# Small work handed out between the blocks of a dense product, and indexer scores on whole 128-row tiles, in a kernel of two small transformers

## The chip, the core and the metric

The kernel runs on one core of a Trainium2 chip, as one program. The metric is the device time of one execution in microseconds. Times of the kernel before and of the changed kernel are medians of several runs. The engines are named as in the profile: PE (TensorE matmul), PEld (its weight loads), DVE (VectorE), ACT (ScalarE), POOL (GpSimd), SP (SyncE, which issues the weight loads from memory).

## The reference

512 tokens of width 1024 in float32 go through two small models, one after the other. The first has two layers: a mixer of convolution and causal attention, a gated linear recurrence, and after each a squared-ReLU MLP of width 4096. The second puts 16 learned meta tokens ahead (528 tokens) and has two layers, each with a hybrid mixer and a gated MLP of width 2816. Only the hybrid mixer is touched in its own code:

```python
def hybrid_mixer(n, w_in, ...):
    proj = n @ w_in          # 528 x 3408 columns
    aq, ak, av, az, aa, ab, bq, bk, bv, iq, ik, iw = jnp.split(proj, SPLIT_POINTS, axis=-1)
    o_a = gated_deltanet(aq, ak, av, az, aa, ab, ...)        # 4 heads of 128, a chunked recurrence
    o_b = dsa_attention(bq, bk, bv, iq, ik, iw, ...)
    gates = sigmoid(n @ w_gate + b_gate)
    return (gates_a * (o_a @ w_branch_a) + gates_b * (o_b @ w_branch_b)) @ w_out

# in dsa_attention: the indexer's scores pick 128 of the real keys for each query
    logit_i = jnp.einsum('bqhd,bsd->bhqs', iqb, ik_r)         # 8 heads of 64
    score = jnp.einsum('bhqs,bqh->bqs', relu(logit_i), iwb)
    _, sel = lax.top_k(score, topk)                           # topk = 128
    p = softmax(concat([s_meta, s_sel]))                      # the 16 meta keys are always seen
    o = p[..., :N_META] @ v_m + p[..., N_META:] @ v_sel
```

## The kernel before

Activations stand with the 128 rows of a block of features on the partitions and the tokens along the free axis. Every dense product is cut into blocks of 128 output columns. Each weight block of 1024 x 128 is loaded by SP's queue into `wraw`, rounded to a short form `whi` by a cast on ACT (L99), and the rest is kept as `wlo` by a subtract on DVE (L100); `whi` and `wlo` have two buffers each. One block of a product over 1024 rows is then 8 steps of 128 rows (the loop over `k` in `products`, L145), each with three matmuls: `whi` by the high part of the activations, `whi` by their low part, `wlo` by the high part. With 528 tokens each matmul is done in two halves, so a block has 48 matmul instructions. Two PSUM tiles `mm` hold running blocks. The evacuation of a block (`evac`) frees its tile.

Around the dense blocks stands small work. Three lists hold it: `fill` (pairs of a cost and a step), `soon`, and `pending`. `product_done` is called once at the end of each block: it runs steps of `fill` until the block's `budget` is spent, then `soon` and one of `pending`, then the evacuation. `issue_after` ties the PE instructions of a step behind a given matmul; instructions of other engines are not tied. The order written here is a rank, not the queue: a planner builds each engine's queue from the ranks with its own modelled times, taking the first in rank that is ready, and the engines then run their queues strictly in order.

The hybrid mixer (`mixer_2`, run twice, called the late mixers here) goes through these stretches:

1. Four blocks of indexer queries (`ev_iq`: an ACT copy, a rotation on DVE L708 to L710, a split into `iq`), then the block of 80 small columns (L814), whose evacuation feeds the indexer's keys. In the first late mixer the normalisation of the stage before ends here too: `sums` (L260), `bc` and `bc1` are one `pending` step each, with a long chain of small DVE instructions and a spread by PE from `diag` (L284).
2. The block of k (`ev_qk`), four of q and one of v. The indexer's keys are turned and split (`keys`, L859, into `ikT[0]` and the low part `ikT[1]`), and `scores` (L880 to L887) come as `fill`: for each of three tiles of queries and each of 8 heads one matmul over 128 rows (L880) and one over the 64 rows that hold the low part (L881), a ReLU on ACT, a multiply-add on DVE.
3. Twelve blocks of the recurrence's q, k and v (`ev_a`: 5 DVE instructions of 528 columns), while `select` (17 steps for each of three tiles; L999 finds the eight largest, L1001 strikes them out, a chain on DVE) and the attention (`attend`) come as `fill` with a budget of 2 a block. What is left is run by `flush`.
4. Four blocks of z and sixteen of gates with the recurrence's preparation (`dn_keys`, `dn_prep`, `dn_solve`, `pair1` to `pair4`), one entry of `steps` a block.
5. The recurrence itself, the two branches, and the output product.

In the attention's `att_values` the 16 meta keys are one matmul of 16 rows (L1067) ahead of the real keys' matmuls of 128 rows (L1070). `squares` sums a block's columns by ten matmuls with one column each (L769).

## Time and profile before

| | |
|---|---|
| three runs, median | 2953.84 us |
| lowest and highest of them | 2943.05 and 2955.46 us |
| the profiled execution, its own time | 2948.39 us |
| its span in the profile | 2946.5 us |
| mean granted TensorE clock | 0.978 |

The profiled execution is one more run. The span is what the trace covers, from the first instruction to the last; 1.9 us of the execution's time lie around it. A granted clock of 1 is TensorE's upper level of 2.4 GHz, 0.5 its lower level of 1.2 GHz, and a number between is a mix of the two over the stretch. The busy time of PE is modelled and holds matmuls that overlap or run slowly, so the distance from start to start says more than the length of one.

### The profile page before, as it was taken

What the parts mean: (1) busy time and instruction counts of PE and PEld (TensorE: products, weight loads), DVE (VectorE), ACT (ScalarE), POOL (GpSimd) and SP (SyncE); (2) the same over time, 40 slices, a digit from 0 to 9 for tenths busy, and PEclk for the clock granted to TensorE, in tenths of its full rate; (3) what the DMA queues carried; (4) which work ended last, traced back from release to release, by engine and by line L of the source; (5) the groups of instructions that cost most, each with busy time, mean ns of one, the idle gap of its engine ahead of it and who ended that gap; (6) DMA issues with size and microseconds to landing.
All of it is one profiled execution on the core that took longest, in us unless ns stands there. A gap on an engine that the chain in (4) does not pass through costs nothing.

```text
span 2946.5 us, 44576 instructions
## 1 busy us (share of the span) xinstructions
PE 2849.4 (97%) x18009; PEld 2505.8 (85%) x18009; DVE 1856.0 (63%) x3462; ACT 1044.0 (35%) x1939; POOL 14.1 (0%) x117
## 2 busy tenths in 40 slices
PE   7999999999999998998999999999999999999999
PEld 5767888877888887888998999999788998988897
DVE  7986535468653557699747564555788757565563
ACT  3444222345321233353633322223444633332222
POOL 0000000000000000000000000000000000000000
PEclk9999999999999999799999999999998999999999
DMA  4214333332333334121354232324221253432333
GB/s 123 65 33 121 93 100 94 100 93 72 99 94 96 98 97 116 45 68 51 109 132 148 86 93 80 101 85 123 58 58 51 82 146 111 116 92 85 104 89 91
DMA packets 509860, 272.23 MB, mean 92 GB/s; under 512 B 40112, under 2 KB 494918, under 8 KB 509398
## 3 DMA queue, kind: packets, MB, share of 16 engines
q1 hardware_dynamic: 493520, 245.24, 29.5%
q10 hardware_dynamic: 16134, 24.14, 2.5%
q8 instruction: 142, 2.33, 0.3%
q14 instruction: 64, 0.52, 0.1%
HBM read 249.11 MB, written 20.23 MB: 91 GB/s over the span
## 4 chain that ended last, share of the span: by engine, by line
PE 87%; DVE 8%; DMA 2%; ACT 1%; issue 1%; SPq 0%; ACTq 0%; DVEq 0%
PE mm L145 74%; PE mm L1449 2%; DVE wlo L100 1%; PE b L1070 1%; PE b L769 1%; PE a L398 1%; PE a L881 1%; DMA qkv<-xz 1%; DVE ac L708 1%; DMA ax<-gd 1%; PE c L423 1%; DVE m L999 1%; DVE ac L971 1%; PE b L1067 1%; PE a L1027 1%
## 5 line engine op out<-in xcount | busy, mean ns | idle before, releaser
L145 PE MATMUL mm<-xparts,whi 128*128 128x256 f32 (+1 forms) x6752 | 1428.5, 320 | 16.8 <-ACT whi L99 7.8
L145 PEld LDWEIGHTS mm<-xparts,whi 128*128 128x128 f32 x6752 | 1045.6, 191 | 115.6 <-issue 9.5
L99 ACT CAST whi<-wraw 128x1024 fp32r<-128x1024 f32 (+1 forms) x472 | 457.8, 970 | 1405.9 <-PE mm L145 1167.8
L145 PE MATMUL mm<-xparts,wlo 128*128 128x256 f32 (+3 forms) x3376 | 888.2, 320 | 11.6 <-DVE wlo L100 11.6
L100 DVE TENSOR_TENSOR wlo<-wraw,whi 128x1024 fp32r<-128x1024 f32 (+1 forms) x472 | 529.3, 1121 | 411.3 <-ACT whi L99 404.9
L145 PEld LDWEIGHTS mm<-xparts,wlo 128*128 128x128 f32 x3376 | 565.4, 191 | 61.8 <-DVE wlo L100 16.7
L145 PE MATMUL mm<-hh,whi 128*128 128x512 f32 (+2 forms) x1040 | 340.1, 354 | 0.0
L145 PE MATMUL mm<-hh,wlo 128*128 128x512 f32 (+2 forms) x1040 | 339.9, 354 | 0.0
L145 PE MATMUL mm<-hl,whi 128*128 128x512 f32 (+2 forms) x1040 | 339.1, 353 | 0.0
L145 PEld LDWEIGHTS mm<-hl,whi 128*128 128x128 f32 x1040 | 184.3, 188 | 27.5
L145 PEld LDWEIGHTS mm<-hh,wlo 128*128 128x128 f32 x1040 | 183.8, 188 | 27.9
L145 PEld LDWEIGHTS mm<-hh,whi 128*128 128x128 f32 x1040 | 184.0, 188 | 26.4
L1449 PE MATMUL mm<-xparts,whi 128*128 128x256 f32 (+2 forms) x512 | 87.6, 289 | 9.2 <-DVE ax L1463 5.0
L507 DVE TENSOR_TENSOR down<-mm,r 128x512 f32<-128x512 f32 x32 | 22.1, 692 | 106.8 <-PE mm L145 106.8
L366 DVE SCALAR_TENSOR_TENSOR val<-z,cw,val 128x512 f32<-128x512 f32 x120 | 84.8, 746 | 0.5
L1449 PEld LDWEIGHTS mm<-xparts,whi 128*128 128x128 f32 x512 | 71.9, 190 | 11.5 <-issue 5.7
L1501 DVE TENSOR_TENSOR fx<-mm,rbc 128x528 f32<-128x528 f32 (+1 forms) x44 | 30.7, 702 | 76.4 <-PE mm L145 76.4
L1514 DVE TENSOR_TENSOR fc<-fc,mm 128x528 f32<-128x528 f32 (+1 forms) x44 | 30.6, 696 | 73.4 <-PE mm L145 73.4
L1102 DVE TENSOR_TENSOR ac<-mm,rbc 128x528 f32<-128x528 f32 (+1 forms) x32 | 22.4, 699 | 77.7 <-PE mm L145 77.7
L145 PE MATMUL mm<-qkv,whi 128*128 128x256 f32 (+2 forms) x384 | 67.6, 284 | 0.0
L1506 DVE SCALAR_TENSOR_TENSOR fc<-fx,vcols,fc 128x528 f32<-128x528 f32 (+1 forms) x88 | 66.1, 757 | 1.4
L1508 ACT ACTIVATE fx<-fc 128x528 f32<-128x528 f32 (+1 forms) x44 | 28.1, 639 | 88.9 <-DVE fc L1506 88.8
(532 smaller groups left out, 3144.0 us busy)
## 6 DMA issues: line engine op xcount, KB each, us to landing
wraw<-in_w_up SPq DMA_DIRECT2D x152, 512.0 KB, 4.0
wraw<-in_w_down SPq DMA_DIRECT2D x96, 512.0 KB, 4.3
wraw<-in_w_in SPq DMA_DIRECT2D x52, 512.0 KB, 3.8
wraw<-in_w_gate SPq DMA_DIRECT2D x32, 512.0 KB, 4.2
wraw<-in_ab_w_in SPq DMA_DIRECT2D x20, 512.0 KB, 3.8
wraw<-in_c_w_in SPq DMA_DIRECT2D x16, 512.0 KB, 3.9
wraw<-in_w_out SPq DMA_DIRECT2D x16, 512.0 KB, 4.8
wraw<-in_w_down SPq DMA_DIRECT2D x32, 192.0 KB, 2.6
```

The costliest lines, as they stand in the source:

```text
L99: self.S.copy(hi[:, :n], raw[:, :n])
L100: self.V.tensor_tensor(lo[:, :n], raw[:, :n], hi[:, :n].bitcast(F32), op=ALU.subtract)
L145: ins = self.PE.matmul(o, lhsT=wt[:, k % chunk, :], rhs=xt[:, t0:t1], start=n == 0, stop=n == 3 * kb - 1)
L366: V.scalar_tensor_tensor(cacc[b], z[b][:, j:j + S], w, cacc[b], op0=ALU.mult, op1=ALU.add)
L398: PE.matmul(ps[:, :W], lhsT=qk[p][r0:r0 + 64, P * i:P * i + P], rhs=qk[4 + p][r0:r0 + 64, :W], start=True, stop=True)
L423: PE.matmul(po[:, 64 * j:64 * j + 64], lhsT=pts[:, P * c:P * c + P], rhs=vt[c][:, h:h + 64], start=c == 0, stop=c == i)
L708: self.V.tensor_tensor(t[o], raw[i], tab[1][i], op=ALU.mult)
L769: PE.matmul(p5[:n, i:i + 1], lhsT=q[:, t0:t0 + n], rhs=self.ones[:, 0:1], start=True, stop=True)
L1449: PE.matmul(o, lhsT=wt[:, k, :], rhs=xt[:, m0 + t0:m0 + t1], start=k == 0 and j == 0, stop=k == 3 and j == 2)
L1501: V.tensor_tensor(x[:, 2:2 + TG], ps, self.rbc, op=ALU.mult)
L1506: V.scalar_tensor_tensor(c, x[:, d + j:TG + j], w(j), c, op0=ALU.mult, op1=ALU.add)
L1514: V.tensor_tensor(c, c, ps, op=ALU.mult)
```

## The change

- `products` now calls `run_fill` after each of the 8 steps of 128 rows instead of once a block, with an eighth of the block's budget. What a step costs beyond its share is carried over as a debt (`credit`), and no more than one share is saved up. Before, each block began anew and the last step could overshoot freely.
- The budgets are set anew: 4.8 a block in the stretch of k, q and v, in which a score costs 1; 4 instead of 2 in the stretch with the selections. An entry of the preparation is cut into its parts, and `dn_prep` into four.
- The cast and the subtract of a weight block get a rank 150 instructions earlier (`high_priority`).
- The low part of the indexer's keys stands in two tiles of 128 rows of which one half is zero (`ikT[1]`, `ikT[2]`), so that L881 takes 128 rows. The meta keys' transposes and matmuls take 128 rows, with zeros in `vt` (tiles of real queries alone). Column sums and transposes of the 16 meta tokens take 128 columns, which saves some small copies.
- The four indexer blocks become two, the block of 80 columns, and two. The block of k comes after them and now has a budget. `bc1` comes one block later, by an empty entry in `pending`.

The core of the diff:

```diff
+AHEAD = 150
@@ weight
-        self.S.copy(hi[:, :n], raw[:, :n])
-        self.V.tensor_tensor(lo[:, :n], raw[:, :n], hi[:, :n].bitcast(F32), op=ALU.subtract)
+        with self.tc.high_priority(AHEAD):
+            self.S.copy(hi[:, :n], raw[:, :n])
+            self.V.tensor_tensor(lo[:, :n], raw[:, :n], hi[:, :n].bitcast(F32), op=ALU.subtract)
@@ products, at the end of each step k
+                self.run_fill(ins, budget / kb)
@@ product_done
         with self.tc.issue_after(ins.ins):
-            self.run_fill(budget)
             for f in soon:
                 f()
@@
-    def run_fill(self, budget):
-        while self.fill and budget > 0:
+    def run_fill(self, ins, budget):
+        self.credit = min(self.credit + budget, budget)
+        while self.fill and self.credit > 0:
             cost, step = self.fill.pop(0)
-            budget -= cost
-            step()
+            self.credit -= cost
+            with self.tc.issue_after(ins.ins):
+                step()
@@ turn_end
-        self.pending = [sums, bc, bc1] + [lambda k=k: final(k) for k in range(0, KB, 2)]
+        self.pending = [sums, bc, lambda: None, bc1] + [lambda k=k: final(k) for k in range(0, KB, 2)]
@@ mixer_2
-                    V.tensor_copy(out[:, :4], p5[:, :4])
-                    V.tensor_copy(out[:META, 4:5], p5[:META, 4:5])
+                    V.tensor_copy(out, p5[:, :5])
...
-            self.dense(w_in[:, 2824:3336], self.xparts, T2, ev_iq, early=True, lag=4)
+            self.dense(w_in[:, 2824:3080], self.xparts, T2, ev_iq, early=True, lag=4)
...
-            self.dense(w_in[:, 2568:2696], self.xparts, T2, ev_qk("k_norm", 4, [kT]))
+            self.dense(w_in[:, 3080:3336], self.xparts, T2, ev_iq, first=2, early=True)
...
-                self.split(ps, *ikT)
-            self.fill.append((99, lambda: None))
-            self.fill.append((0.5, keys))
+                S_.copy(ikT[0], ps)
+                for i in range(2):
+                    o = slice(64 * i, 64 * i + 64)
+                    V.tensor_tensor(ikT[1 + i][o], ps[o], ikT[0][o].bitcast(F32), op=ALU.subtract)
+            BS_ = 4.8
+            self.fill.append((BS_, lambda: None))
+            self.fill.append((1, keys))
+            self.fill.append((2, lambda: None))
...
-                PE.matmul(ps[:, :W], lhsT=q[r0:r0 + 64], rhs=ikT[1][r0:r0 + 64, :W], start=False, stop=True)
+                PE.matmul(ps[:, :W], lhsT=q, rhs=ikT[1 + h % 2][:, :W], start=False, stop=True)
...
-                    self.fill.append((0.25 + 0.14 * i, lambda i=i, h=h: scores(i, h)))
-            self.dense(w_in[:, 2056:2568], self.xparts, T2, ev_qk("q_norm", 0, qT), budget=4.5)
-            self.dense(w_in[:, 2696:2824], self.xparts, T2, ev_v, budget=4.5)
+                    self.fill.append((1, lambda i=i, h=h: scores(i, h)))
+            self.dense(w_in[:, 2568:2696], self.xparts, T2, ev_qk("k_norm", 4, [kT]), budget=BS_)
+            self.dense(w_in[:, 2056:2568], self.xparts, T2, ev_qk("q_norm", 0, qT), budget=BS_)
+            self.dense(w_in[:, 2696:2824], self.xparts, T2, ev_v, budget=BS_)
...
-                    PE.matmul(po[:, j, :], lhsT=vt[:META, 4, :], rhs=tm[:, :n], start=True, stop=W == META)
+                    PE.matmul(po[:, j, :], lhsT=vt[:META if W == META else P, 4, :], rhs=tm[:, :n], start=True, stop=W == META)
...
-                self.dense(col(w_in, b), self.xparts, T2, ev_a, first=b, budget=2)
+                self.dense(col(w_in, b), self.xparts, T2, ev_a, first=b, budget=4)
...
-            steps += [[lambda t=t: dn_prep(*t)] for t in tiles[1:]]
-            steps.append([lambda: dn_prep(*tiles[0]), dn_solve])
+            gens = [dn_prep(*t) for t in tiles]
+            part = lambda i: lambda: next(gens[i], None)
+            steps += [[part(i)] * 4 for i in range(1, 5)]
+            steps.append([part(0)] * 4 + [dn_solve])
...
-                    self.fill.append((1, lambda k=k: [f() for f in steps[k]]))
+                    self.fill.extend((1 / len(steps[k]), f) for f in steps[k])
```

## Rows read from the trace of the kernel before

**Rows 1.** The page, part 1: each engine's busy time over the whole span.

```profile
PE 2849.4 (97%) x18009; PEld 2505.8 (85%) x18009; DVE 1856.0 (63%) x3462; ACT 1044.0 (35%) x1939; POOL 14.1 (0%) x117
```

**Rows 2.** Windows: stretch, length, busy time per engine (instructions), granted clock, DMA share, GB/s.

```profile
1128.60:1179.70 51.10, 44.35 (x317) 40.87 (x318) 41.00 (x82) 16.25 (x27) 0.98 (x5) 0.87 0.43 126
1179.70:1254.20 74.50, 73.65 (x400) 59.79 (x398) 47.57 (x124) 27.42 (x52) 0.79 (x5) 0.79 0.16 43
1254.20:1343.00 88.80, 83.86 (x643) 77.87 (x641) 82.88 (x199) 45.91 (x103) 1.00 (x10) 1.00 0.22 60
1343.00:1400.00 57.00, 50.92 (x353) 46.76 (x353) 51.36 (x106) 18.88 (x41) 0.00 (x0) 0.91 0.20 56
1750.00:1800.00 50.00, 50.00 (x415) 50.00 (x414) 27.84 (x38) 13.56 (x16) 0.40 (x4) 1.00 0.25 74
2047.20:2090.10 42.90, 38.94 (x309) 37.00 (x308) 34.07 (x60) 15.85 (x25) 0.46 (x7) 1.00 0.34 89
2090.10:2159.50 69.40, 68.97 (x399) 55.79 (x397) 47.50 (x124) 27.23 (x52) 0.86 (x5) 0.85 0.17 46
```

**Rows 3.** Timeline of PE, first products of the first late mixer: start, length.

```profile
1155.49 2.04 PE L284 MATMUL a<-diag,ones 128*128 128x512 f32 x2 [1.02 <-DVE diag L271]
1160.83 0.81 PE L145 MATMUL mm<-xparts,wlo 128*128 128x256 f32 x2 [3.30 <-DVE wlo L100]
```

**Rows 4.** Timeline of PE, the indexer's scores of the first late mixer.

```profile
1200.12 0.28 PE L880 MATMUL a<-ikT,iq 128*128 128x256 f32 x1
1200.34 0.38 PE L881 MATMUL a<-ikT,iq 64*128 64x256 f32 x1
1200.65 0.39 PE L145 MATMUL mm<-xparts,whi 128*128 128x256 f32 x1
1233.05 0.39 PE L880 MATMUL a<-ikT,iq 128*128 128x512 f32 x1
1233.37 0.61 PE L881 MATMUL a<-ikT,iq 64*128 64x512 f32 x1
```

**Rows 5.** Windows of three stalls and their ends, columns as in rows 2.

```profile
1148.70:1160.80 12.10, 5.43 (x11) 2.07 (x10) 11.67 (x24) 3.32 (x7) 0.21 (x2) 0.62 0.00 0
1349.00:1356.40 7.40, 7.40 (x31) 6.54 (x32) 6.61 (x16) 1.16 (x4) 0.00 (x0) 0.50 0.51 143
2256.00:2266.00 10.00, 10.00 (x37) 8.26 (x37) 6.38 (x14) 1.59 (x6) 0.00 (x0) 0.50 0.38 107
```

**Rows 6.** Timeline of PE at the end of the q, k and v blocks.

```profile
1340.15 1.45 PE L145 MATMUL mm<-xparts,whi 128*128 128x256 f32 x8
1342.81 1.18 PE L769 MATMUL b<-ones,sqq 128*16 128x1 f32 x10 [1.21 <-ACT sqq L764]
1348.92 2.00 PE L769 MATMUL b<-ones,sqq 128*16 128x1 f32 x10 [4.93 <-ACT sqq L764]
```

**Rows 7.** Timeline of DVE in the same stretch.

```profile
1342.46 0.75 DVE L971 SCALAR_TENSOR_TENSOR ac<-ax,vcols,ac 128x528 f32<-128x528 f32 x1
1343.20 0.55 DVE L1001 MATCH_REPLACE8 selw<-m,selw 128x384 f32<-128x384 f32 x1
1348.99 1.19 DVE L100 TENSOR_TENSOR wlo<-wraw,whi 128x1024 fp32r<-128x1024 f32 x1
```

**Rows 8.** DVE's groups of instructions between 1343 and 1450 us.

```profile
L999 DVE MAX8 m<-selw 128x8 f32<-128x512 f32 (+1 forms) x16 | 10.9, 681 | 0.2
L1001 DVE MATCH_REPLACE8 selw<-m,selw 128x512 f32<-128x512 f32 (+1 forms) x15 | 10.0, 667 | 0.0
```

**Rows 9.** Waits over the whole span: us, times, longest us.

```profile
ACT whi L99 <- PE mm L145: 1167.8, 353, 6.9
PE mm L145 <- DVE wlo L100: 11.6, 9, 3.3
```

**Rows 10.** Timeline of PE, values of the attention, a meta-key pair and real keys.

```profile
1371.10 0.48 PE L1067 MATMUL b<-ptm,vt 16*128 16x128 f32 x2
1371.51 0.94 PE L1070 MATMUL b<-ptr,vt 128*128 128x128 f32 x6
```

More of the change, by code (lines that the diff above doesn't have):

```diff
@@ L40, in __init__ @@
         self.n = 0
+        self.credit = 0
         self.vec, self.ahead = {}, []
@@ L147, in run @@
                     n += 1
+                self.run_fill(ins, budget / kb)
             state[i][-1] = n
             if n == 3 * kb:
-                self.product_done(ins, lambda: evac(view), early, budget)
+                self.product_done(ins, lambda: evac(view), early)
         if n and not lead and kb <= KB:
@@ L167, in products, with product_done @@
             run(i, order)
-    def product_done(self, ins, evac, early=False, budget=0):
+    def product_done(self, ins, evac, early=False):
         soon, self.soon = self.soon, []
         with self.tc.issue_after(ins.ins):
-            self.run_fill(budget)
             for f in soon:
@@ L198, in flush @@
             f()
-        self.run_fill(math.inf)
+        while self.fill:
+            self.fill.pop(0)[1]()
+        self.credit = 0
     def need_r(self):
@@ L258, in col_sums @@
         ps = self.aux()
+        nt = 4 if T == S else 5
         for i, t0, n in self.tok_tiles(T):
-            self.PE.matmul(ps[:n, i:i + 1], lhsT=acc[:, t0:t0 + n], rhs=self.ones[:, 0:1], start=True, stop=True)
+            self.PE.matmul(ps[:, i:i + 1], lhsT=acc[:, t0:t0 + P], rhs=self.ones[:, 0:1], start=True, stop=True)
         c = self.t(self.sp, [P, 5], "csum")
-        if T != S:
-            self.G.memset(c, 1.0)
-            self.V.tensor_scalar(c[:T - S, 4:5], ps[:T - S, 4:5], scale, bias, op0=ALU.mult, op1=ALU.add)
-        self.V.tensor_scalar(c[:, :4], ps[:, :4], scale, bias, op0=ALU.mult, op1=ALU.add)
-        return c if T != S else c[:, :4]
+        self.V.tensor_scalar(c[:, :nt], ps[:, :nt], scale, bias, op0=ALU.mult, op1=ALU.add)
+        return c[:, :nt]
     def diag(self, r, T):
@@ L289, in spread @@
             n = T - S
-            self.PE.matmul(pm[:, :n], lhsT=self.ones[:n, :], rhs=dm, start=True, stop=True)
+            self.PE.matmul(pm[:, :n], lhsT=self.ones, rhs=dm, start=True, stop=True)
             self.S.copy(bc[:, :n], pm[:, :n])
@@ L768, in sums @@
                     for i, t0, n in tiles:
-                        PE.matmul(p5[:n, i:i + 1], lhsT=q[:, t0:t0 + n], rhs=self.ones[:, 0:1], start=True, stop=True)
-                    V.tensor_copy(out[:, :4], p5[:, :4])
-                    V.tensor_copy(out[:META, 4:5], p5[:META, 4:5])
+                        PE.matmul(p5[:, i:i + 1], lhsT=q[:, t0:t0 + P], rhs=self.ones[:, 0:1], start=True, stop=True)
+                    V.tensor_copy(out, p5[:, :5])
                 self.soon.append(sums)
@@ L853, in mixer_2 @@
             V.tensor_copy(ikr[:, :, 1, :], ikr[:, :, 0, :])
-            ikT = [self.t(ip, [P, S], f"ikT{i}", F32R) for i in range(2)]
+            ikT = [self.t(ip, [P, S], f"ikT{i}", F32R) for i in range(3)]
+            for i in range(2):
+                G.memset(ikT[1 + i][64 - 64 * i:128 - 64 * i, :].bitcast(F32), 0.0)
             def keys():
@@ L859, in keys @@
                     PE.transpose(ps[:, P * i:P * i + P], ikr[:, i].rearrange("p a b -> p (a b)"), self.ident)
-                self.split(ps, *ikT)
-            self.fill.append((99, lambda: None))
-            self.fill.append((0.5, keys))
+                S_.copy(ikT[0], ps)
+                for i in range(2):
+                    o = slice(64 * i, 64 * i + 64)
[4 more added lines that the diff above has]
+            self.fill.append((2, lambda: None))
             rr = self.t(sm, [P, 5], "rr")
@@ L1071, in att_values, with attend @@
                                       start=False, stop=c == i)
-                for j, h in enumerate(hs):
-                    S_.copy(ob[h][:, t0:t0 + n], po[:, j, :])
+                S_.copy(ob[h][:, t0:t0 + n], po[:, j, :])
             units = [{"t": t, "hs": (h, h + 1)} for t in tiles for h in (0, 2)]
-            def attend(k):
+            def attend(k, cost):
+                fs = []
+                if k < len(units):
+                    fs.append(lambda: att_scores(units[k]))
                 if k >= 2:
-                    att_values(units[k - 2])
-                if k < len(units):
-                    att_scores(units[k])
+                    fs += [lambda j=j: att_values(units[k - 2], j) for j in range(2)]
                 if 1 <= k <= len(units):
-                    att_turn(units[k - 1])
+                    fs.append(lambda: att_turn(units[k - 1]))
+                fill.extend((cost / len(fs), f) for f in fs)
             fill = self.fill
@@ L1089, in mixer_2 @@
                     if i == 1 and it in (3, 7, 11, 15):
-                        fill.append((0.5, lambda k=it // 4: attend(k)))
+                        attend(it // 4, 0.5)
                 for k in (2 * i + 2, 2 * i + 3):
                     if i < 3:
-                        fill.append((0.5 + 0.4 * i, lambda k=k: attend(k)))
+                        attend(k, 0.5 + 0.4 * i)
             for k in range(8, 12):
-                fill.append((2.0, lambda k=k: attend(k)))
+                attend(k, 2.0)
             gd = self.gd
```

34 lines of the change are left out of this document (20 added, 14 removed).

## The prediction

> **What bounds the kernel now.** I read the totals first: PE is busy for 97% of the span and DVE for 63% [rows 1], so time can come from places where PE stands still or runs slowly, and the whole page hides those. The next view was a table of stretches. A stretch of the MLP shows what PE does undisturbed: 415 matmuls of half a token range in 50 us, 0.1205 us from start to start, clock 1.00 [rows 2]; a block of 48 takes 5.78 us. Against this the late mixers fall short in three places. In the first stretch of the first mixer the clock is 0.87 and PE is busy 44.4 of 51.1 us. In the blocks of k, q and v PE looks full, 73.7 of 74.5 us, yet retires 400 instructions, at a clock of 0.79; in the second mixer 399 in 69.4 us at 0.85. In the stretch of the selections DVE is busy 82.9 of 88.8 us and PE 83.9, so the two are close to even and neither can be loaded more for nothing [rows 2]. Then I read PE's timeline in each of these, and DVE's beside it.
>
> **The change part by part.** The sum goes against the profiled execution, 2948.39 us; it is 5.5 us under the median of the runs, which spread by 12 us, and 0.5% (15 us) is about what a measurement can tell from no change.
>
> *Scores (widening, spreading, the new budget).* Six blocks need 6 x 5.78 = 34.7 us. Five groups of column sums at 1.18 us [rows 6] are 5.9, and I allow 1.5 for the few transposes. That leaves 74.5 - 42.1 = 32.4 us for 24 scores in the first mixer and 69.4 - 42.1 = 27.3 in the second. In the changed kernel a score is two matmuls over 128 rows. Such a one goes from start to start in 0.22 us with 256 columns and 0.32 with 512 [rows 4], on average 0.27, so a score costs 0.54 as an upper bound. The lower bound is the pace of the dense blocks, 0.12 per 256 columns, or 0.36 for two of 384. I take 0.46, nearer the upper row since single small matmuls stand between dense ones: 11 us for 24. Available are 21 + 16 = 37 us. The clock holds most of it: a mean of 0.79 is the lower level for 42% of 74.5 us, 31 us, and half of that, 15.6, is lost; 0.85 loses 10.4 of 69.4 [rows 2]. So 26 us are clock and 11 are the half-height matmuls and what follows them. At the upper level the matmul over 64 rows takes 0.31 us to the next start where the one over 128 rows takes 0.22, with equal columns [rows 4]; taking it to 128 rows saves at least 0.09 a score, 4 us in all, and more where the next dense block's matmul is late as well.
>
> That the clock comes back is an inference. It falls after scores that stand almost alone, and in the dense stretches and in the selections, where small matmuls stand between dense ones, it is 1.00 [rows 2]. Handed out at 0.6 of a score per step of six dense matmuls, the scores stand between dense ones too. The cover that this needs is DVE: from 1128.6 to 1254.2 us it works 88.6 us, and if these 125.6 us shrink to some 95, DVE is 93% full, as it is in the selections, where PE lost 4.9 of 88.8 us to it [rows 2]. I charge the same 5.5% of 95 us, 5 us in each mixer. Sum: -37 + 10 = **-27** (bounds -10, clock left low, and -37).
>
> *First stretch.* In 12.1 us PE does 11 instructions [rows 5]. They need 2.9 us: two spreads at half of the 2.04 us that one takes at the lower clock [rows 3], and seven at the dense pace. PE waits for `diag` and then 3.3 us for a `wlo` [rows 3], which stood behind rotations on DVE. The stretch's clock of 0.87 is 13 us at the lower level [rows 2]; 9 of them lie in the stall (0.62 of 12.1 us, [rows 5]), and the other 4 cost 2 us. In all 11 us are lost. The earlier rank removes the wait for `wlo`; the two indexer blocks instead of four, and `bc1` a block later, take rotations out of the way of the chain behind `diag`. That chain is still long and shares DVE, so I leave 3 us standing: -8. In the second mixer PE idles 4.0 of 42.9 us [rows 2] and I take -2. Sum **-10** (bounds -3 and -13).
>
> *End of the selections' blocks.* After eight matmuls that need `whi` alone PE waits 1.2 and 4.9 us behind column sums [rows 6]; the next dense block could not go on, since its `wlo` was cut at 1348.99 though its `whi` was used from 1340.15 on. On DVE an instruction of the evacuation and one of the selection take turns meanwhile, each waiting for its own predecessor [rows 7], and the subtract ranks behind both. With its rank 150 earlier it goes first, and PE has the dense block to do while the sums ripen. The stall costs 6.1 us and 7.4 us at the lower clock, 3.7 lost; in the second mixer the lower clock lasts 10 us [rows 5], and I take the stall for the same. Of some 20 us I take **-12**: DVE is 90% busy from 1343 to 1400 us [rows 2] and will not let PE have all (bounds 0 and -20).
>
> *Budget 4 in the selections.* Before, with 2 a block and a fresh start at each, steps of 2.0 to 2.7 are handed out per block, 34.9 of cost in twelve blocks by the list's own costs; after, 4 x 12 = 48. The further 13.1 are selections of the third tile, 1.2 for one of 0.68 + 0.67 us [rows 8]: 14.7 us of DVE work per mixer that moves ahead of evacuations in a stretch that DVE fills to 93%. At worst PE loses all of it, 29 us for both. At best nothing, because the turns on DVE are set by each chain waiting for itself and stay one to one. I take **+10**, nearer the second, since rows 7 show the turns (bounds 0 and +29).
>
> *Meta keys.* A pair over 16 rows takes 0.41 us to the next start, a pair over 128 rows about 0.94 / 3 = 0.31 [rows 10]. Some 32 such pairs: 3 us, of which part lies where DVE sets the pace: **-2** (0 to -4). The transposes that grow to 128 columns cost PE what their neighbours cost; no change taken.
>
> *The rest.* Waits of PE for `wlo` are 11.6 us in all [rows 9], 3.3 of them counted above. The preparation's steps come up to a block earlier. The saved small DVE copies are some 0.15 us each. **-5** (0 to -9). In the MLPs PE never waits, so their weights' new rank gives nothing there; the two zeroed halves and the cleared `vt` lie on POOL, which is idle.
>
> Sum: 2948.4 - 27 - 10 - 12 + 10 - 2 - 5 = **2902 us**.
>
> **A rule against the widening.** The row says that height costs time: 0.31 us against 0.22 [rows 4]. The Trainium skill's page "TensorE: Matmul & The Clock Gate", section "Why this matters for your kernels", has a matmul of few rows take as long as one of 128, and sees the gain of a small height in tiles that run side by side; the trace disagrees on the first, since here 64 rows take longer than 128. By that rule the widening saves nothing, and the sum would be that of the second rival.
>
> **The rivals.**
> *Clock stays low.* If it falls for another reason than the lone scores, 20 of the 26 us of clock stay: 2922. Against it: 1.00 in the selections, with their small matmuls.
> *Height costs nothing.* Then the 11 us that are not clock stay: 2913. The row of 0.31 speaks against it; that the next dense matmul then starts late could have another cause.
> *Fill rate.* The budget costs PE its full 29 us instead of 10: 2921. For it: DVE at 93% in that stretch. With a low clock besides: 2941.
> *Nothing new.* The planner builds the queues, and the scores already stand singly between dense matmuls [rows 4]. If spreading and rank only shuffle equal orders, a few us of the widening remain: 2943.
> *Slower: casts first.* Queues run in order. ACT already waits 353 times, 1167.8 us, for PE to release `whi` [rows 9]. A cast moved up stands in front of copies, ReLUs and squares, and the subtract in front of the DVE instruction that frees PSUM. Where PE in turn needs that evacuation, a block loses the wait in front of the cast, on average 1167.8 / 353 = 3.3 us. It decides once 14 of the some 80 blocks in the mixers lose this (14 x 3.3 = 46 us, the gain); at a third of them, 27 blocks, 2991. The same page, section on the array's architectural detail, calls ACT and DVE strict queues; the trace agrees by ACT's 1167.8 us of waiting. Against it: DVE and ACT mostly have slack in the MLPs, and the planner issues a cast only when its model sees the buffer free.
>
> **How the numbers follow.** Forecast 0.52 (2880 to 2912 as its own range, by half the distance to the bounds of the larger terms), height 0.06, low clock 0.12, fill rate 0.10, both 0.05, nothing new 0.08, slower 0.07. The range must reach from below the forecast's own range, 2868 (every saving near its bound), to 2945, past all but the slower case. Faster by over 0.5% of the median is under 2939: forecast, height, low clock, fill rate and a part of the both-case, 0.82. Within 0.5%: the rest of it and nothing new, 0.11. Slower: 0.07.
>
> **What would show it.** Right: in the changed profile the k, q and v stretches last some 53 to 58 us each at a clock above 0.95; the matmuls over 64 rows are gone; PE's wait of 4.9 us after the recurrence's last blocks is gone and the subtract there runs right after its cast; PE has fewer waits for `wlo`. Wrong: a clock again under 0.9 in the scores, a longer stretch of the twelve blocks with DVE full and PE under 90%, or ACT's waits for PE longer, with relus and copies behind casts.

## The result and the profile after

The changed kernel takes 2915.98 us (median of 4 runs, 2911.97 to 2916.99) against 2954.65 us for the kernel before, measured beside it (median of 4, 2943.05 to 2959.7): ratio 0.9872, 95% interval 0.9841 to 0.9903, so 1.3% faster, beyond its interval. The forecast was 2902 us, 14 us too low, in a range of 2868 to 2945. The profiled execution took 2915.08 us, 33.3 us less than the one profiled before; its span is 2913.3 us.

The page, part 1, of the changed kernel, answers to [rows 1]:

```profile
PE 2811.8 (97%) x18009; PEld 2496.7 (86%) x18009; DVE 1851.5 (64%) x3442; ACT 1045.0 (36%) x1939; POOL 16.3 (1%) x117
```

PE retires the same 18009 instructions in 37.6 us less busy time; its share of the span is the same. As before, only windows show where the time went. The same view as [rows 2] (busy times in the order PE, PEld, DVE, ACT, POOL), now cut at the first evacuation of `ev_a`; the block of k lies in the first stretch in both kernels, so the second holds four blocks of q, one of v and the first of `ev_a`:

```profile
1128.60:1171.20 42.60, 39.53 (x318) 38.31 (x318) 34.32 (x74) 15.51 (x25) 1.38 (x6) 1.00 0.38 112
1171.20:1230.60 59.40, 57.55 (x426) 56.01 (x425) 54.11 (x132) 28.89 (x53) 1.82 (x8) 0.94 0.29 86
1230.60:1336.60 106.00, 97.40 (x697) 88.64 (x696) 98.09 (x236) 51.15 (x122) 1.01 (x10) 0.95 0.20 56
2030.30:2069.70 39.40, 37.66 (x309) 36.97 (x308) 31.87 (x62) 14.63 (x23) 0.55 (x7) 1.00 0.36 99
2069.70:2122.60 52.90, 51.77 (x400) 49.83 (x399) 49.34 (x124) 28.20 (x53) 0.87 (x5) 1.00 0.23 63
```

The first stretch shrank from 51.1 and 42.9 us to 42.6 and 39.4, the second from 74.5 and 69.4 to 59.4 and 52.9, with the clock up from 0.79 and 0.85 to 0.94 and 1.00: 43.6 us in all. In the third DVE is busy for 98.1 of 106 us, and there the time goes the other way. The evacuations of `ev_a` and of the gates by source line, with the first and the last start; the kernel before, first mixer, and then the changed one, both mixers:

```profile
L966 DVE TENSOR_TENSOR ax<-mm,rbc x12: 685/704/708, 1254.4 to 1340.0; 128x528 f32<-128x528 f32 x12
L1102 DVE TENSOR_TENSOR ac<-mm,rbc x16: 684/708/710, 1399.8 to 1528.4; 128x528 f32<-128x528 f32 x16
```

```profile
L979 DVE TENSOR_TENSOR ax<-mm,rbc x12: 687/694/706, 1230.8 to 1336.6; 128x528 f32<-128x528 f32 x12
L1120 DVE TENSOR_TENSOR ac<-mm,rbc x16: 695/708/709, 1401.3 to 1512.2; 128x528 f32<-128x528 f32 x16
L979 DVE TENSOR_TENSOR ax<-mm,rbc x12: 684/698/703, 2122.8 to 2227.3; 128x528 f32<-128x528 f32 x12
L1120 DVE TENSOR_TENSOR ac<-mm,rbc x16: 685/696/697, 2291.1 to 2402.7; 128x516 f32<-128x516 f32 x16
```

In the first mixer the twelve evacuations span 105.8 us where they spanned 85.6 (+20.2), and from the last of them to the last gate it is 175.6 us instead of 188.4 (-12.8). In the second mixer the same two are +19.0 (before 2159.8 to 2245.3) and -15.9 (last gate before at 2436.6). So -43.6 + 39.2 - 28.7 = -33.1 us: the whole difference lies in the late mixers, and 39 us of it were paid and only partly given back.

PE's timeline at the end of the twelve blocks, in place of [rows 6]:

```profile
1337.40 0.71 PE L148 MATMUL mm<-xparts,whi 128*128 128x256 f32 x4 [0.84 <-DVE ax L979]
1339.41 1.62 PE L775 MATMUL b<-ones,sqq 128*128 128x1 f32 x10 [1.30 <-ACT sqq L770]
1345.62 0.81 PE L148 MATMUL mm<-xparts,wlo 128*128 128x256 f32 x2 [4.59 <-DVE wlo L103]
```

The stall that was to go is still there, under another name: 1.30 and 4.59 us instead of 1.21 and 4.93, now for a `wlo`. ACT had cast that block at 1329.42; DVE cut it at 1344.36, and worked nearly all of the time between. Over the whole span, waits as in [rows 9]:

```profile
ACT whi L102 <- PE mm L148: 1125.5, 335, 8.6
PE mm L148 <- DVE wlo L103: 9.2, 2, 4.6
```

Nine waits for a `wlo` have become two, one at the end of these blocks in each mixer. ACT waits 42 us less for PE, not more.

### The profile page after: what moved, and what is told of

It is laid out like the page before. It is cut to its first block, busy times and chain, and to the rows that moved or that the text cites. A ratio compares the mean times of both kernels' runs of the same rounds, so it can differ in the third digit from the quotient of the medians.

```text
span 2913.3 us, 44557 instructions
## 1 busy us (share of the span) xinstructions
PE 2811.8 (97%) x18009; PEld 2496.7 (86%) x18009; DVE 1851.5 (64%) x3442; ACT 1045.0 (36%) x1939; POOL 16.3 (1%) x117
## 4 chain that ended last, share of the span: by engine, by line
PE 83%; DVE 11%; ACT 2%; DMA 2%; issue 1%; SPq 0%; ACTq 0%; DVEq 0%
PE mm L148 72%; PE mm L1473 2%; DVE wlo L103 2%; DVE ac L714 1%; DVE ac L984 1%; DVE m L1012 1%; PE a L404 1%; DVE selw L1014 1%; PE b L775 1%; PE c L429 1%; ACT whi L102 1%; PE b L1087 0%; DMA qkv<-xz 0%; DMA xz<-x 0%; DMA ax<-gd 0%
## 5 line engine op out<-in xcount | busy, mean ns | idle before, releaser
L102 ACT CAST whi<-wraw 128x1024 fp32r<-128x1024 f32 (+1 forms) x472 | 457.5, 970 | 1359.0 <-PE mm L148 1125.5
```

The costliest lines, as they stand in the source:

```text
L102: self.S.copy(hi[:, :n], raw[:, :n])
```

## The experiments

All twelve start from the changed kernel but one, which starts from the kernel before. The interval of a ratio is 0.1 to 0.3% to either side, so two kernels that are less than some 10 us apart are told apart by their traces, not by their times. The last column subtracts medians of different sessions; by the ratios it comes out the same within some 2 us.

| run | us, median | ratio to before (95%) | against 2916 |
|---|---|---|---|
| changed kernel | 2916.0 | 0.9872 (0.9841 to 0.9903) | |
| budget 3 | 2907.7 | 0.9840 (0.9820 to 0.9860) | -8 |
| no rank | 2930.3 | 0.9920 (0.9900 to 0.9939) | +14 |
| 64-row scores | 2936.1 | 0.9941 (0.9919 to 0.9963) | +20 |
| fill once a block | 2918.3 | 0.9879 (0.9861 to 0.9897) | +2 |
| 64 rows, fill once a block | 2937.3 | 0.9947 (0.9929 to 0.9965) | +21 |
| scores' part undone, but for the order of the indexer's blocks | 2953.9 | 1.0005 (0.9997 to 1.0014) | +38 |
| meta keys' part undone | 2940.3 | 0.9953 (0.9938 to 0.9968) | +24 |
| meta values alone undone | 2928.3 | 0.9914 (0.9898 to 0.9930) | +12 |
| budget 2 | 2904.4 | 0.9832 (0.9810 to 0.9853) | -12 |
| rank alone on the kernel before | 2952.5 | 0.9994 (0.9984 to 1.0004) | |
| rank 400 | 2918.4 | 0.9886 (0.9865 to 0.9906) | +2 |
| budget 2, rank 400 | 2888.2 | 0.9781 (0.9768 to 0.9795) | -28 |

**Height of the scores' second matmul.**

```diff
-                PE.matmul(ps[:, :W], lhsT=q, rhs=ikT[1 + h % 2][:, :W], start=False, stop=True)
+                r0 = 64 * (h % 2)
+                PE.matmul(ps[:, :W], lhsT=q[r0:r0 + 64], rhs=ikT[1 + h % 2][r0:r0 + 64, :W], start=False, stop=True)
```

> The changed kernel, but the second matmul of each indexer score again over the 64 rows that hold its head's low part, as in the kernel before; spreading, budget and rank stay changed. 48 such matmuls in the program. (a) By the row of before (0.31 us from start to start against 0.22 with equal columns) this costs at least 0.09 us each, 4.3 us, and with what the next dense block's matmul then waits, 0.19 at most (0.31 against the 0.12 of the changed kernel), 9 us: 2920 to 2925 us, clock in the k, q and v blocks still above 0.93. (b) Rival, height costs nothing: within 2 us of 2916, and the two matmuls of a score at equal distances. (c) Rival, the half-height matmuls are themselves what brought the clock down: the clock in these blocks falls under 0.88 and the time goes to 2935 or more.

2936 us, twice the upper expectation. PE's timeline of one score over 384 columns with 64 rows, and then PEld's, the weight loads:

```profile
2119.01 0.34 PE L892 MATMUL a<-ikT,iq 128*128 128x384 f32 x1
2119.27 0.44 PE L894 MATMUL a<-ikT,iq 64*128 64x384 f32 x1
2119.65 0.51 PE L148 MATMUL mm<-xparts,whi 128*128 128x256 f32 x2
```

```profile
2118.88 0.19 PEld L892 LDWEIGHTS a<-ikT,iq 128*128 128x128 f32 x1
2119.27 0.18 PEld L894 LDWEIGHTS a<-ikT,iq 64*128 64x128 f32 x1 [0.20 <-issue]
2119.64 0.30 PEld L148 LDWEIGHTS mm<-xparts,whi 128*128 128x128 f32 x2 [0.19 <-issue]
```

and PE's and PEld's in the changed kernel:

```profile
2103.86 0.34 PE L892 MATMUL a<-ikT,iq 128*128 128x384 f32 x1
2104.03 0.34 PE L893 MATMUL a<-ikT,iq 128*128 128x384 f32 x1
2104.21 1.17 PE L775 MATMUL b<-ones,sqq 128*128 128x1 f32 x10
2106.29 0.40 PE L892 MATMUL a<-ikT,iq 128*128 128x512 f32 x1
2106.53 0.39 PE L893 MATMUL a<-ikT,iq 128*128 128x512 f32 x1
```

```profile
2106.17 0.19 PEld L892 LDWEIGHTS a<-ikT,iq 128*128 128x128 f32 x1
2106.30 0.19 PEld L893 LDWEIGHTS a<-ikT,iq 128*128 128x128 f32 x1
```

With whole tiles the next weights are loaded 0.23 us ahead of their matmul (2106.30 and 2106.53), beside the one in flight. With 64 rows the load starts when its matmul does (2119.27), and so does the load of the 128-row tile behind it: both changes of height are paid. A score of 384 columns takes 0.64 us instead of 0.35, and 0.29 x 48 = 14 us. This fits what "Key Properties" on the Trainium skill's page "TensorEngine Tiling (Array Packing)" says, that a change of the tiling mode drains the engine; it names no price. From the first score to the first evacuation of `ev_a` the windows say the same, 37.5 and 36.1 us after, 43.1 and 44.1 here, 13.6 us more. The 37.5 were at a clock of 0.91, the other three at 1.00; at one clock it would be some 17 us. The rest of the 20 us is less than the runs can tell.

**Spreading, height and density.** First the filling once per block, whole tiles kept; then that with 64 rows; then the old costs, budget and relu tile as well ("all undone" below; the order of the indexer's blocks stays new):

```diff
-                self.run_fill(ins, budget / kb)
             state[i][-1] = n
             if n == 3 * kb:
+                self.run_fill(ins, budget)
```

```diff
-            BS_ = 4.8
+            BS_ = 4.5
             self.fill.append((BS_, lambda: None))
-            self.fill.append((1, keys))
-            self.fill.append((2, lambda: None))
+            self.fill.append((0.5, keys))
...
-                t = self.t(self.sp, [P, T2], "sq")
+                t = self.t(wk, [P, T2], "sqq")[:, :512]
...
-                    self.fill.append((1, lambda i=i, h=h: scores(i, h)))
+                    self.fill.append((0.25 + 0.14 * i, lambda i=i, h=h: scores(i, h)))
```

> The changed kernel with the small work handed out once, at the end of each dense block with the block's whole budget, instead of after each sixth matmul; whole tiles, rank and budgets stay changed. (a) My inference: scores in lumps stand nearly alone and wait for one another's evacuation, and that is why the clock fell; then the clock of the k, q and v blocks falls to 0.79 to 0.88 again and some 20 of the 26 us of clock return, 2936 us. (b) Rival, the height did it (64 rows against 128): the clock stays above 0.93 and the time within 5 us of 2916. (c) Rival, the planner deals single steps out evenly in any case: instruction order nearly equal, within 3 us of 2916.

> The changed kernel with two of its parts taken back at once: the second matmul of each score over 64 rows, and the small work handed out once per dense block. Alone, the first cost 20 us at a clock of 1.00 in the k, q and v blocks, the second 2 us, also at 1.00. (a) The clock falls only where both come together: 64-row matmuls that keep the array waiting, in lumps. Then these blocks show 0.79 to 0.88 as before, and the time is 2936 and some 15 to 25 us of clock: 2951 to 2961 us. (b) The two are independent and the low clock of the kernel before came from the old order of the indexer's blocks or the tile of the relu: clock above 0.93 and 2936 to 2941 us.

> The changed kernel with all of the scores' part but the order of the indexer's blocks taken back: 64-row second matmuls, work handed out once per block, costs of 0.39, 0.53 and 0.67 a score at a budget of 4.5 (some eight scores a block, where the changed kernel gives about five), the relu in the tile that the squares use. With 64 rows and one handing out per block alone, 2937 us and a clock of 0.97 and 0.92 in the k, q and v blocks. (a) Dense lumps of 64-row matmuls bring the clock down: 0.79 to 0.88 there and 2945 to 2955 us. (b) The clock of the kernel before came from its order of blocks or its 16-column sums: clock 0.92 or more and 2933 to 2941 us.

Windows from the first score to the first evacuation of `ev_a`, second mixer, in six kernels: before; changed; filled once a block; 64 rows; 64 rows filled once a block; all undone.

```profile
2108.20:2159.70 51.50, 51.07 (x250) 38.37 (x250) 30.95 (x68) 20.09 (x40) 0.86 (x5) 0.80 0.14 39
```

```profile
2086.70:2122.80 36.10, 36.09 (x269) 34.36 (x269) 32.94 (x80) 18.99 (x39) 0.87 (x5) 1.00 0.22 59
```

```profile
2086.90:2123.70 36.80, 36.78 (x274) 34.96 (x273) 31.64 (x74) 19.15 (x39) 1.15 (x5) 1.00 0.21 58
```

```profile
2098.40:2142.50 44.10, 44.10 (x269) 34.91 (x268) 33.53 (x79) 19.27 (x39) 0.86 (x5) 1.00 0.17 48
```

```profile
2096.30:2144.60 48.30, 48.30 (x269) 37.65 (x268) 32.00 (x73) 19.35 (x39) 0.86 (x5) 0.89 0.17 44
```

```profile
2106.60:2165.90 59.30, 58.50 (x289) 45.05 (x290) 37.88 (x84) 22.44 (x43) 0.64 (x5) 0.77 0.13 36
```

PE is full in all six, but PEld is not: 34 to 35 of 36 to 37 us with whole tiles, 35 to 45 of 44 to 59 with 64 rows. Spreading alone is worth 2 us, which is nothing, and the run without it says little of the clock, since the planner deals the scores out by itself. Between the first and the last score PE's timeline has some 126 and 155 dense matmuls in that run (first and second mixer), nearly as many as in the changed kernel (126 and 153), in that with 64 rows (121 and 150) and in that with 64 rows filled once a block (124 and 158). In the kernel before it has 88 and 84, with all undone 75 and 75. So it is the new costs and budget, five scores a block instead of eight, that put the scores further apart.

The clock goes with both height and distance. At the new distance 64-row tiles keep 1.00 when spread and show 0.96 and 0.89 when filled once a block, where whole tiles in nearly the same order keep 1.00. At the old distance and with 64 rows it is 0.73 and 0.80 (before) and 0.76 and 0.77 (all undone). No run put whole tiles at the old distance, so whether the distance alone would have brought the clock back stays open.

With all undone the time is that of the kernel before, but not by the same road: there the first twelve scores stand behind one another, 24 matmuls without a dense one between them, where the kernel before has six at most, and the keys came too early, so that PE waited 6.4 and 1.7 us for them (for `ikr`, in its timeline). The lower clock began in the first of these waits and, in the second mixer, some 3 us behind the other. The changed kernel has such a wait too, 1.68 us in the first mixer, and a clock of 0.51 from 1193.3 to 1200 us, just behind it, with whole tiles; that is its 0.91 there. A fall while PE was busy throughout shows with 64 rows filled once a block, in the first two lines here; in the third the clock stays low among the scores with all undone:

```profile
2115.00:2120.00 5.00, 5.00 (x31) 3.78 (x29) 1.42 (x3) 3.02 (x5) 0.00 (x0) 1.00 0.00 0
2120.00:2125.00 5.00, 5.00 (x22) 3.83 (x22) 4.54 (x8) 1.58 (x3) 0.15 (x1) 0.66 0.40 105
2116.00:2126.00 10.00, 10.00 (x28) 6.66 (x28) 5.27 (x11) 3.90 (x8) 0.00 (x0) 0.50 0.00 0
```

**Meta keys.** The whole part back to 16 rows and 16 columns (the core of it), then the values alone, the last pair of lines:

```diff
-                    PE.matmul(p5[:, i:i + 1], lhsT=q[:, t0:t0 + P], rhs=self.ones[:, 0:1], start=True, stop=True)
-                V.tensor_copy(out, p5[:, :5])
+                    PE.matmul(p5[:n, i:i + 1], lhsT=q[:, t0:t0 + n], rhs=self.ones[:, 0:1], start=True, stop=True)
+                V.tensor_copy(out[:, :4], p5[:, :4])
+                V.tensor_copy(out[:META, 4:5], p5[:META, 4:5])
...
-                m = META if W == META else P
+                m = META
...
-                    PE.matmul(po[:, j, :], lhsT=vt[:META if W == META else P, 4, :], rhs=tm[:, :n], start=True, stop=W == META)
+                    PE.matmul(po[:, j, :], lhsT=vt[:META, 4, :], rhs=tm[:META, :n], start=True, stop=W == META)
```

> The changed kernel with the meta keys' part taken back: the attention's values and transposes, the column sums and the spreads of the 16 meta tokens use 16 rows or 16 columns again, with the small copies and clears that go with it. Scores, spreading, rank and budgets stay changed. (a) On record: 2 us (0 to 4), 2916 to 2920 us. (b) After the run with half-height scores, where a 64-row matmul among 128-row ones cost 20 us for 48, or 0.4 us each, and the weight load before and after it no longer ran beside the matmul in flight: there are some 64 matmuls and transposes of 16 rows or 16 columns in the attention and some 100 in the sums; if a small tile costs by its rows alone, the 32 values matmuls give 32 x 0.4 = 13 us, 2929 us; if columns count too, up to 2940 us and more. (c) No cost, because DVE sets the pace where they stand: 2914 to 2918 us.

> The changed kernel with one thing of the meta keys' part taken back: the attention's values product of the meta keys over 16 rows again, 32 pairs of matmuls in the program; transposes, sums, spreads and small copies stay changed. With the whole part taken back the time was 24 us longer, and in that run a pair over 16 rows and what surrounds it took 0.25 to 0.3 us more than over 128. (a) Rows are the cost: 32 x 0.3 = 10 us, 2926 us, and the other 14 us belong to the sums and transposes of 16 columns, the extra small DVE instructions and the clock. (b) Rows and the clock that follows them are all of it: 2935 us or more. (c) On record: 2918 us, the 24 us come from elsewhere.

24 and 12 us, where 2 were on record. PE's timeline of one head's values, with 16 rows, and below it in the changed kernel:

```profile
1380.68 0.60 PE L1071 MATMUL b<-ident,s 128*128 128x128 f32 x4
1381.21 0.48 PE L1084 MATMUL b<-ptm,vt 16*128 16x128 f32 x2
1381.62 1.16 PE L1087 MATMUL b<-ptr,vt 128*128 128x128 f32 x8
1382.54 0.49 PE L148 MATMUL mm<-xparts,wlo 128*128 128x256 f32 x2
```

```profile
1374.93 0.60 PE L1071 MATMUL b<-ident,s 128*128 128x128 f32 x4
1375.36 0.41 PE L1084 MATMUL b<-ptm,vt 128*128 128x128 f32 x2
1375.62 1.06 PE L1087 MATMUL b<-ptr,vt 128*128 128x128 f32 x8
1376.43 0.49 PE L148 MATMUL mm<-xparts,wlo 128*128 128x256 f32 x2
```

From the transposes ahead to the dense matmul behind it is 1.86 us against 1.50, at a clock of 1.00 in both. The pair itself takes 0.15 of the 0.36 more (0.41 against 0.26), the approach 0.10 and the way back 0.11. For all 32 pairs this would be 11.5 us, about what was measured, but that they agree is luck: half of the pairs stand in the twelve blocks, and these are no longer with 16 rows (105.9 and 104.5 us from the first evacuation to the last, against 105.8 and 104.5). The time is lost behind them, and there the lower clock lasts longer. The same length of the first mixer, with 16 rows and below it in the changed kernel:

```profile
1335.30:1401.00 65.70, 58.87 (x368) 54.19 (x368) 44.28 (x104) 32.88 (x105) 0.00 (x0) 0.79 0.14 41
1336.60:1402.30 65.70, 58.91 (x436) 56.21 (x437) 50.13 (x121) 40.63 (x130) 0.00 (x0) 0.90 0.16 47
```

In the second mixer it is 0.82 against 0.90. A clock lower by 0.11 and 0.08 over some 66 us is worth 7 and 5 us; the 16 pairs that stand there are worth 6 by the 0.36. The two overlap, and no run parts them. The other 12 us of this part lie with the sums, spreads and transposes of 16 columns and the small DVE copies; which of them, no run told.

**Rank.** Taken out of the changed kernel, and, the other way round, put alone into the kernel before:

```diff
-        with self.tc.high_priority(AHEAD):
-            self.S.copy(hi[:, :n], raw[:, :n])
-            self.V.tensor_tensor(lo[:, :n], raw[:, :n], hi[:, :n].bitcast(F32), op=ALU.subtract)
+        self.S.copy(hi[:, :n], raw[:, :n])
+        self.V.tensor_tensor(lo[:, :n], raw[:, :n], hi[:, :n].bitcast(F32), op=ALU.subtract)
```

> The changed kernel with the rank of the weight cast and subtract taken back (both stand where the program writes them); all else stays changed. (a) My sum: the rank is part of the term for the first stretch (-10), of the term for the end of the selections' blocks (-12) and of the rest (-5). The stall of 4.6 us at the end of those blocks is still in the changed kernel, so the second of these did not come; what is left is 8 to 15 us: 2924 to 2931 us, with a wait of 3 us for a wlo behind the spreads again. (b) Rival, the queues' order follows from when the buffers come free and not from the rank: within 4 us of 2916, and the orders on ACT and DVE nearly equal. (c) Rival, casts first: the rank puts casts ahead of evacuations and costs; without it 2900 us or less, and ACT's wait for PE shorter than 1125 us.

> The kernel before with the rank of the weight cast and subtract alone (150 earlier); scores, spreading, budgets, order of blocks and meta keys as before. (a) On record: the rank takes the greater part of the first stretch's -10, all of the -12 at the end of the selections' blocks and most of the rest's -5: about -24, so 2929 us against 2953, with the wait of 4.93 us behind the last column sums gone. (b) From the run without it: 14 us, 2939 us; the wait at the end is gone too, as the budget of 2 leaves DVE the time. (c) The rank does nothing by itself or puts casts in the way: 2950 us or more, wait still there.

Without it the changed kernel is 14 us longer. Its waits for `wlo`, and from PE's timeline the longest of them in the first mixer, ahead of the scores:

```profile
PE mm L147 <- DVE wlo L102: 23.2, 8, 5.9
```

```profile
1188.70 0.81 PE L147 MATMUL mm<-xparts,wlo 128*128 128x256 f32 x2 [5.88 <-DVE wlo L102]
```

The next longest, 5.40 us, stands within the twelve blocks of each mixer, whose evacuations span 114.2 and 115.9 us there instead of 105.8 and 104.5. At the end of the blocks the wait is 2.06 us, shorter than the 4.59 with the rank.

Alone on the kernel before it gives nothing, 0.9994. PE no longer waits there for these `wlo`, and waits for others that stood behind them:

```profile
1171.75 0.73 PE L815 MATMUL mm<-xparts,wlo 128*80 128x256 f32 x2 [7.11 <-DVE wlo L809]
1349.42 2.01 PE L770 MATMUL b<-ones,sqq 128*16 128x1 f32 x10 [5.05 <-ACT sqq L765]
```

The first is the block of 80 columns, whose cast and subtract are written out by hand and got no rank. The second is the stall of [rows 6], unmoved: DVE's work was put in another order and there was as much of it.

**Budget and rank together.** A budget of 3, then of 2, then 2 with the higher rank, then that rank alone:

```diff
-                self.dense(col(w_in, b), self.xparts, T2, ev_a, first=b, budget=4)
+                self.dense(col(w_in, b), self.xparts, T2, ev_a, first=b, budget=2)
...
-AHEAD = 150
+AHEAD = 400
```

> The changed kernel with the budget of the twelve blocks of ev_a at 3 instead of 4, which hands out nearly what the kernel before did there (36 of cost against 34.9); all else stays changed. In the changed kernel these twelve blocks last 20.2 and 19.0 us longer than before, and the stretch behind them 12.8 and 15.9 us less. (a) My sum: the earlier work is paid for mostly but not all given back, +10 us for the budget; then this kernel takes 2916 - 10 = 2906 us, the twelve blocks fall back to some 86 us and the stretch behind them grows by some 14 us each. (b) Rival, full price: 29 us are lost to the budget, 2887 us. (c) Rival, a plain shift of DVE work from one place to another: within 4 us of 2916.

> The changed kernel with the budget of the twelve blocks of ev_a at 2. At 3 it took 2907.7 us, PE's wait of 4.6 us for a wlo at the end of these blocks was gone, DVE was busy 91.5 of 98.0 us in them and 56.2 of 70.0 us behind them, PE 89.9 and 68.7. (a) The stretch in which DVE is short is still these blocks: another 12 of cost moves out of them, and at half the effect of the step from 4 to 3 the time is 2903 to 2906 us. (b) The work that is left (24 of some 75 handed out) piles up behind the blocks and the attention becomes late for the gates and the branch: 2912 us or more. (c) Even: 2907 to 2909 us.

> The changed kernel with the budget of the twelve blocks of ev_a at 2 and the rank of the weight cast and subtract 400 earlier instead of 150. With a budget of 2 and 150 the time was 2904.4 us, PE waited 3.73 us for a wlo right after these blocks, where the rest of the selections is put in line at once, and the lower clock followed for some 10 us. (a) The rest of the selections outranks the subtract there and 400 puts it first: the wait goes, and with it 4 to 6 us in each mixer, 2893 to 2897 us. (b) The order on DVE follows from when buffers come free in the planner's reckoning and not from the rank: wait still there, 2902 to 2907 us. (c) Casts this early stand in the way of copies and squares elsewhere: 2910 us or more.

> The changed kernel with the rank of the weight cast and subtract 400 earlier instead of 150, its budget of 4 in the twelve blocks of ev_a kept. It closes the square of rank and budget: 150 and 4 took 2916 us, 150 and 2 took 2904, 400 and 2 took 2888. (a) The subtract at the end of these blocks was late for want of rank: with 400 the wait of 4.6 us goes here too, as do the slow microseconds behind it, 2898 to 2905 us; what the budget costs beside that stays. (b) It was late because DVE is behind its plan in these blocks (93% busy): the wait stays and 2912 to 2918 us; rank helps only once the budget has freed DVE.

With rank 400 and a budget of 4 the waits for a `wlo` are gone and PE waits for evacuations and squares in their place: 12.5 us for the former instead of the changed kernel's 6.2, 5.1 for the latter instead of 2.6. With budget 2 and rank 150 a `wlo` is late once more where the rest of the selections is put in line. First PE's waits in the former, then its timeline in the latter:

```profile
PE mm L148 <- DVE ax L979: 12.5, 8, 4.1
```

```profile
1316.67 0.81 PE L148 MATMUL mm<-xparts,wlo 128*128 128x256 f32 x2 [3.73 <-DVE wlo L103]
```

Windows of the twelve blocks and of what follows them, with a budget of 2, first with rank 150 and then with 400:

```profile
1230.60:1312.00 81.40, 79.35 (x614) 74.81 (x613) 76.10 (x181) 44.78 (x102) 1.02 (x10) 1.00 0.24 65
1312.00:1401.00 89.00, 84.09 (x636) 80.77 (x636) 74.67 (x172) 46.54 (x138) 0.00 (x0) 0.92 0.22 63
```

```profile
1230.30:1306.00 75.70, 75.17 (x582) 71.07 (x581) 72.89 (x165) 41.27 (x93) 1.01 (x10) 1.00 0.26 70
1312.00:1401.00 89.00, 87.63 (x690) 83.11 (x689) 74.76 (x170) 48.49 (x137) 0.00 (x0) 1.00 0.23 69
```

The twelve evacuations of the first mixer span 105.8, 95.3 and 78.9 us with budgets of 4, 3 and 2 at rank 150. Rank 400 instead of 150 is worth nothing at a budget of 4 (2916 and 2918 us) and 16 us at 2 (2904 and 2888). At 4 the stall at the end of the blocks stays in the first mixer, now 4.11 us for a square; at 2 no `wlo` is waited for and no lower clock follows, 1.00 against 0.92. DVE's share of the twelve blocks is no lower at a budget of 2 (76.10 of 81.4 us and 72.89 of 75.7, against 98.09 of 106.0): it has less to do there, and not more time left. The last kernel beats both, 28 us under the changed one and 2.2% under the kernel before.

## Why the prediction came out as it did

**Scores, -27: right in size, its cause shown in part.** The stretches of q and v with the first of `ev_a` were forecast at 53 to 58 us with a clock above 0.95; they are 59.4 and 52.9 at 0.94 and 1.00, just outside, and 31.6 us less than before. The step "It falls after scores that stand almost alone" is borne out as far as it was tried: with 126 and 153 dense matmuls between the scores instead of 88 and 84 the clock came back, with 64 rows too (1.00 in both mixers). But it leaves out the height, for in nearly the same order whole tiles show 1.00 where 64 rows show 0.96 and 0.89. And the handing out in steps had no part in it: once per block, the planner puts the scores in nearly the same places. The height was also undersized, at 11 us in the sum, 4 of them from the spacing of one matmul; undone by itself it is 20, of which the trace shows 14 to 17, because the load behind the short tile is exposed as well as its own. With that the price of a score fell to the lower bound, a mean of 0.12, 0.17 and 0.24 twice, 0.35 us, where 0.46 was taken.

**First stretch, -10: right,** 12.0 us. The wait of 3.3 us for a `wlo` behind the spread is gone. That the rank removed it is not shown: without the rank PE does not wait for a `wlo` there either, but 5.88 us for one further on, ahead of the scores.

**End of the selections' blocks, -12: failed.** The step was that the subtract, "With its rank 150 earlier", goes first. It did not, nor did it with the rank alone. With rank 400 it did, and PE waited 6.3 us more for evacuations and 2.5 more for squares instead of 9.2 for a `wlo`. DVE is 93% busy there, and the order of its queue chose which wait shows; with a budget of 3 PE's longest wait for a `wlo` there is 0.5 us at rank 150, with 2 it is 3.73 us again, and with 2 and rank 400 there is none. Why DVE's queue comes out so, no run told.

**Meta keys, -2: the worst-sized term.** It is 24 by undoing it, and between the first evacuation of `ev_a` and the last gate the two mixers are 18 us longer in that trace. The forecast took the pair's own spacing, 0.41 against 0.31, and left out the way in and out, the lower clock behind the twelve blocks, and the sums and transposes altogether ("no change taken").

**Budget, +10: right in size by undoing it** (8 us with 3, 12 with 2, both about what the intervals can tell), **wrong in its sum and as a term of one.** By the list's own costs the kernel before hands out 29.8 in the twelve blocks and not 34.9, which twelve blocks of at most 2.7 cannot reach; the changed kernel hands out 48.1, so 18.3 more: 13.2 of selections of the third tile, 2.5 for the last step of the second and 2.6 of attention. Budgets of 2 and 3 hand out 24.4 and 36.1, to either side of the kernel before. Behind the first evacuation of `ev_a` the terms -12, +10, -2 and -5 were to give -9. That part came out at +39.2 - 28.7 = +10.5, although the meta keys brought 18 there. In the traces a budget of 2 gives back 12.6 us of it and one of 3 nothing; what made up the rest, no run told. The budget and the stall are not two terms: with the rank at 400, where no `wlo` is late, going from a budget of 2 to 4 costs 30 us (2888 and 2918) instead of 12. So the total is 13 us short of the forecast: 6.6 better in the first two stretches, 19.5 worse behind them. That it still came this near is in part luck, since the meta keys brought 22 more than their term while the stall stayed and the moved work cost more than the sum had.

**The rest, -5,** can't be told apart from the rank's 14 us, which are spread over three terms. The parts undone one at a time, 38 + 24 + 14 - 12 (budget at 2), make 64 us and not 38: each leaves behind a state in which the others weigh differently, as the rank's 2 us on the kernel before and 14 here show.

**The rivals.** Height costs nothing: no; the short matmul does not merely take as long as the tall one, its neighbours wait for it. Clock stays low: no. Nothing new: half true, for the planner does deal the scores out by itself, and the spreading is worth 2 us; the gain lies in the tiles and in the new costs and budget of the scores. Casts first: no, ACT's waits for PE fell from 1167.8 to 1125.5 us, and 400 costs no more than 150. The fill rate did cost what that rival feared at the place, 39 us, before the later stretch gave back most of it. Of the signs of being wrong one came in part: the twelve blocks are longer with DVE 93% busy, but PE is at 92% and not under 90%.

## What to carry to other kernels

Look at PEld beside PE: where a weight load no longer starts ahead of its matmul, look for a change of tile height, and price it over the whole way from the full-height matmul ahead to the one behind; a few zero rows are cheaper. Before work is moved into a stretch, ask which engine it loads there: in a stretch that DVE filled, a higher rank renamed the wait (2916 and 2918 us), and the same rank was worth 16 us once half of the work handed out there was taken away. Terms that draw on the same engine are not to be added up. And before a run counts as one with the old order, look in its trace whether the order is the old one: here one run kept nearly the new order, and another got one that neither kernel had.

## What the runs showed of the hardware that was not expected

A 64-row matmul between 128-row ones cost 0.29 us more than a whole one of the same columns, which takes 0.17, and, in one place at a clock of 1.00, a pair of 16 rows 0.36 us more than one of 128; weight loads at both borders of the 64-row matmul lost their cover. The granted clock fell in a stretch in which PE counts as busy all the time: with 64-row scores filled once a block from 1.00 to 0.66 between two stretches of 5 us with PE busy 5.00 of 5.00 and PEld 3.8. With the scores packed closer it was 0.50 over 10 us with PE busy 10.00 of 10.00 and PEld 6.66. With whole tiles in the order of the former it was 1.00, PEld busy 35 of 37 us. Which of the two, the loads without cover or the half-filled array, the clock answers to, the runs do not tell.
